# Input projection, third column pair as a seven-product block, and the attention spread over fewer units

## The chip, the cores and the metric

The kernel runs on one core of a Trainium2 chip. Its engines are TensorE (PE, the matmuls), VectorE (DVE), ScalarE (ACT), GpSimd (POOL) and SyncE (SP, which here only issues transfers); each works through its own instructions in order, and they wait for each other by semaphores. The metric is the time of one execution on the device in microseconds, lower is better.

## The reference

One encoder layer for 512 tokens of width 2048, all in float32:

```python
h = rmsnorm(x, g_mix)
qa, ka, va, qb, kb, vb = split(h @ w_in)          # 8 x 128, 2 x 128, 2 x 128, then three times 8 x 128
out_a = rmsnorm(mixer_a(qa, ka, va, g_q_a, g_k_a), g_out_a)   # 8 query heads on 2 kv heads, q/k normed, rotary
out_b = rmsnorm(mixer_b(qb, kb, vb), g_out_b)                 # 8 heads, three dilated windows, partial rotary
x = x + concat(out_a, out_b) @ w_out              # 2048 x 2048
h2 = rmsnorm(x, g_ffn)
x = x + (silu(h2 @ w_gate) * (h2 @ w_up)) @ w_down            # 5632 wide
return rmsnorm(x, g_final)
```

## The kernel before

**Number format.** A float32 product is made of three matmuls: each operand is split into a high part (ACT copies it to the 128x512 fp32r tile) and a low part (DVE subtracts the high part from the source), and `mm3` (L238 to L240) multiplies high by high, high by low and low by high. So each weight tile costs ACT and DVE one operation each, and those of DVE must be done before PE comes to the tile.

**Units.** The program is a list of units, one per weight tile, and the main loop issues them in order: it loads tiles ahead, splits some ahead, issues the unit's matmuls, then hooks that hang on that unit, and then tasks from a queue called `side`. Two kinds of unit occur in the part of concern. A plain unit (`in_chunk`, weights called `w`) takes 128 rows of the weights by 512 columns against all four groups of 128 tokens: 12 matmuls, 16 units for a chunk of 512 columns. A block unit (`ColBlock`, weights called `tw`) belongs to a scheme of seven products that computes a pair of chunks with 7/8 of the multiplications: 8 pairs of row groups x 7 products = 56 units of 6 matmuls, where two plain chunks would take 32 units of 12. A block needs sums and differences of raw weight tiles, which DVE makes (L825), and evicts its results in parts which are added up.

**Order of the program.** 16 units of a first chunk (kvA), block 1 (qA0, qA1, units 16 to 71), block 2 (vB0, vB1, units 72 to 127), then four plain chunks qkB0 to qkB3 (units 128 to 191), each with 256 columns of q and 256 of k of two B heads; then the output projection of the A heads (out A, 4 chunks of 8 units, 192 to 223) and of the B heads (out B, 224 to 255), then the feed-forward blocks, three quarters of the time. The chunk results that attention needs later go to DRAM (`store`) and are read back (`reload`, `load_vB`).

**Attention** has no units of its own. `attention_tasks` makes a queue of some 140 tasks with costs, in one order: the rotary tables (L410, L416), the q ropes of heads 0 to 3 (`norm_rope`, L432 to L449, on DVE), the split of vA (L492), the k ropes, then head 0's q transposes (L547) and the k transposes (L500), and then the slots. A slot (`head_slot`) is one step of a pipeline over heads: the score of 128 queries (three matmuls, L238 to L240 on `qT`), the norm of the slot before, the transposes of four p tiles six slots behind (L594, split into `pTh` and `pTl`), the exponential, and the product with v eight slots behind. The A heads take slots 0 to 31, the B heads 32 to 63. The q ropes of heads 4 to 7 hang on slots 6 to 9. How fast the queue is drained is set by numbers:

```python
credit = credit + HEAD_RATE[n >= attend[1]] if attend[0] <= n < attend[2] else 1.0
while side and credit >= getattr(side[0], "cost", 1.0):
    f = side.popleft()
    credit -= getattr(f, "cost", 1.0)
    f()
```

Before, `HEAD_RATE` gives 1.42 per unit beside the plain chunks and 1.9 beside out A. An A slot costs 1.5 and a B slot 1.2, so that up to two fit into a unit now and then. Eight PSUM banks are handed out in rotation (`bank`, `release`): a score of an A head keeps its bank until the exponential has read it, one of a B head until one DVE operation has, and the p transposes keep theirs until `pTl` is written (L230).

The o tiles of the A heads and of six B heads are stored to DRAM (`o_dram`) and read back by `Back` beside the first output chunk; the other B heads' are split by `early` just ahead of the units that use them. The arena holds the operands of the seven-product scheme; parts of it are reused by name (`place(m, i)`) when a form is no longer read.

Of the kernel before, what the change touches and what calls it, by code (L numbers as in the profile page):

```python
# [47 lines left out]
PLAIN_WAIT = 5  # L48
SPILL_B = 6
TWINS = 8  # L50
# [5 lines left out]
EVICT = 6  # L56
HEAD_RATE = (1.42, 1.9)
TURN_LAG = 6
VALUE_LAG = 8
COLUMN_BLOCKS = 2  # L60

# [6 lines left out]
def encoder_block(ctx, tc, x, g_mix, w_in, g_q_a, g_k_a, g_out_a, g_out_b, w_out, g_ffn,  # L68
# [31 lines left out]
    def release(*tiles):  # L100
        banks.extend(tiles)
# [54 lines left out]
    def place(m, i):  # L156
# [3 lines left out]
    O_HOMES = {"A": [(m, i) for i in range(6) for m in (5, 6)] + [(3, i) for i in range(4)],  # L160
               "B": [(m, i) for i in (6, 7) for m in range(7)]}

    load_x(0)
# [225 lines left out]
    def make_r1():  # L389
        ss = small()  # L390
        nc.vector.tensor_reduce(ss, x_ss.rearrange("p (t c) -> p t c", t=NT), axis=AX.X, op=OP.add)
        r1["r"] = rsqrt_mean(ss, NT, D)
        r1["rs"] = small()
        nc.vector.tensor_scalar(r1["rs"], r1["r"], HD ** -0.5, None, op0=OP.mult)

# [67 lines left out]
    def row_scale_of(name):  # L463
        return r1["rs" if name[:2] == "qB" else "r"]

    def post_plain(name, ps, rows=range(NT)):
        for t in rows:
            e = homes.popleft() if name == "kvA" else slot("ev" + name)
            if name[:3] == "qkB":
                nc.scalar.activation(e[:, :256], ps[t][:, :256], AF.Copy, scale=r1["rs"][:, t:t + 1])  # L470
                nc.scalar.activation(e[:, 256:], ps[t][:, 256:], AF.Copy, scale=r1["r"][:, t:t + 1])
            else:
                nc.scalar.activation(e, ps[t], AF.Copy, scale=1.0 if name == "kvA" else r1["r"][:, t:t + 1])
            release(ps[t])
            store(name, t, e)
            if name == "kvA":
                homes.append(e)
# [33 lines left out]
    def split_vB(h):  # L511
        vB[h] = split(vB[h].rearrange("p t c -> p (t c)"), "v")

    turn = [0]

    def rope_partial(q0, t):
# [4 lines left out]
        for s in range(2):  # L521
# [7 lines left out]
    o_dram = {(g, h): dp.tile([P, 512], F32, tag=f"o{g}{h}", name=f"o{g}{h}")  # L529
              for g, n in (("A", NHA), ("B", SPILL_B)) for h in range(n)}  # L530
    acc = {}
    heads = []

    class Head:
# [5 lines left out]
        def tq(self):  # L540
            ps = bank()
            for t in range(NT):
                if self.kind == "A":
                    src = qA[self.h // 4][t][:, (self.h % 4) * HD:(self.h % 4 + 1) * HD]
                else:
                    src = qkB[self.h // 2][t][:, (self.h % 2) * HD:(self.h % 2 + 1) * HD]
                nc.tensor.transpose(ps[:, t * P:(t + 1) * P], src, ident)  # L547
            self.q = split(ps, "qT")
            release(ps)

        def tk(self):
            if self.kind == "A":
                self.k = kTA[self.h // (NHA // NKV)]
                return
            ps = bank()
            for t in range(NT):
                lo = 256 + (self.h % 2) * HD
                nc.tensor.transpose(ps[:, t * P:(t + 1) * P], qkB[self.h // 2][t][:, lo:lo + HD], ident)
            self.k = split(ps, "kT")
            release(ps)  # L560

        def score(self, t):
# [46 lines left out]
        def fin(self):  # L609
            o = slot("oT")  # L610
            nc.scalar.activation(o, self.o, AF.Copy)
            oT[self.kind, self.h] = o
            if self.kind == "A" or self.h < SPILL_B:
                nc.gpsimd.dma_start(o_dram[self.kind, self.h], o)
# [178 lines left out]
    class ColBlock:  # L793
        def __init__(self, w, row, lo, pairs, plan, tag, ready=None, close=None, chain=CHAIN, apart=False):
# [6 lines left out]
            def raw(i, j, q):  # L801
                at = row + (2 * q + i) * P
                return Raw(lambda t: [(w[0, at:at + P, lo[j]:lo[j] + 512], t)], tag=tag, width=512)
            kinds = {"a": (0, 0), "b": (0, 1), "c": (1, 1), "d": (1, 0), "e": (0, 1), "f": (1, 0), "g": (1, 1)}
# [93 lines left out]

    def in_plain(name, lo):
        pieces = [(QB + 256 * lo, 0, 256), (KB + 256 * lo, 256, 256)] if name[:3] == "qkB" else [(lo, 0, 512)]  # L900
        in_chunk(pieces, lambda ps, rows: post_plain(name, ps, rows))

    first_chunk(1024, lambda ps: post_plain("kvA", ps))
    groups = [(("qA0", "qA1"), (0, 512)), (("vB0", "vB1"), (VB, VB + 512)), (("qkB0", "qkB1"), (0, 1)),
              (("qkB2", "qkB3"), (2, 3))]
    for names, lo in groups[:COLUMN_BLOCKS]:
# [24 lines left out]
    def out_chunk(kind, c):  # L931
# [4 lines left out]
        def early(k):  # L936
            if (kind, k) not in oS:
                drain_until(lambda: (kind, k) in oT)
                oS[kind, k] = split(oT.pop((kind, k)), "oS", go[:, base + k:base + k + 1],
                                    at=O_HOMES["B"][2 * k:2 * k + 2] if k < 7 else None)  # L940

# [29 lines left out]
        def post(rows):  # L971
# [9 lines left out]
            if kind == "B" and NT - 1 in rows:  # L981
# [10 lines left out]
                for i in (2 * c, 2 * c + 1):  # L992
# [3 lines left out]
        add_chunk(w_out, [(base + k) * P for k in order], [(c * 512, 0, 512)], mm, None,  # L996
                  early if kind == "B" else None,
                  (lambda k: [Back(k)] if kind == "A" or k < SPILL_B else []) if c == 0 else None, tag="wa" if kind == "A" else "wo")

# [429 lines left out]
```

## Time and profile before

| | |
|---|---|
| three runs, median | 1996.75 us (1995.93 to 1997.94) |
| the profiled execution | 1996.41 us, of which its trace spans 1994.6 |
| PE busy | 1978.2 us (99%) |
| DVE, ACT, POOL busy | 1560.1, 1108.2, 146.8 us |
| moved to and from DRAM | 390.62 MB, mean 196 GB/s |

Times in the profile are in microseconds from the span's start. In a row of a timeline stand the start, the duration, the engine, the line, the operation, what it writes and reads with the tile's size, and in brackets how long the engine had been idle and on what it waited. Matmuls are pipelined: a row's duration is longer than the distance to the next one, and the distance is what a matmul costs. Rows by stretch give the busy time of engines between two points in time. The units of block 2 end at 212.56 us, the first p is transposed at 274.1, and the last result of the plain chunks goes to DRAM from 466.5.

### The profile page before, as it was taken

The page shows a single profiled execution, that of the slowest core. Times are in us where ns is not written, and L with a number is a line of the kernel's source. Part 1 is how long each engine was busy: PE and PEld are TensorE (multiplying, and loading weights), DVE is VectorE, ACT ScalarE, POOL GpSimd, SP SyncE. Part 2 cuts the span into 40 slices and gives each one's busy share as a digit, 9 for nine tenths or more (in the row PEclk, how much of TensorE's full clock was granted, in tenths as well). Part 3 has the DMA queues.
Part 4 walks back from the last instruction along what each step waited for, and adds up shares of the span by engine and source line. Part 5 has one row for each costly group of instructions (what it writes and reads, how often), then busy time and mean ns, then how long its engine had stood idle before and what let it go on. Part 6 is the DMA issues. An engine that isn't in the chain of part 4 may idle for free. (4 is left out here: it accounts for less than half of the span.)

```text
span 1994.6 us, 27480 instructions
## 1 busy us (share of the span) xinstructions
PE 1978.2 (99%) x9019; PEld 1631.7 (82%) x9019; DVE 1560.1 (78%) x2786; ACT 1108.2 (56%) x1984; POOL 146.8 (7%) x191
## 2 busy tenths in 40 slices
PE   9999999999999999999999999999999999999997
PEld 7888888888888888888888888888888888788886
DVE  6888866668845698877878877878779987887968
ACT  7655345546543565555554555545556666666655
POOL 0000111101110000000000000000000121111121
PEclk9999999999999999999999999999999999999999
DMA  8586532335353654845837647658458699768864
GB/s 276 180 279 233 174 122 94 111 118 195 100 174 100 212 180 166 288 145 214 287 117 257 236 141 277 201 181 282 151 199 279 193 247 269 196 167 269 196 171 156
DMA packets 229216, 390.62 MB, mean 196 GB/s; under 512 B 21408, under 2 KB 70352, under 8 KB 228944
## 3 DMA queue, kind: packets, MB, share of 16 engines
q1 hardware_dynamic: 204736, 325.87, 48.6%
q0 software_dynamic: 17680, 41.95, 9.3%
q10 hardware_dynamic: 6656, 21.05, 3.1%
q8 instruction: 70, 1.15, 0.2%
q14 instruction: 74, 0.61, 0.1%
HBM read 325.08 MB, written 63.70 MB: 195 GB/s over the span
## 5 line engine op out<-in xcount | busy, mean ns | idle before, releaser
L238 PE MATMUL b<-tw,arena 128*128 128x512 f32 x2136 | 837.9, 392 | 2.2 <-ACT ev L1168 2.2
L239 PE MATMUL b<-tw,arena 128*128 128x512 f32 x2136 | 832.5, 390 | 1.9 <-DVE tw L788 1.8
L240 PE MATMUL b<-tw,arena 128*128 128x512 f32 x2136 | 832.4, 390 | 0.0
L785 ACT ACTIVATE tw<-raw 128x512 fp32r<-128x512 f32 x924 | 559.1, 628 | 437.0 <-DVE raw L825 283.9
L788 DVE TENSOR_TENSOR tw<-raw,tw 128x512 fp32r<-128x512 f32 x924 | 620.8, 689 | 171.4 <-ACT tw L785 168.2
L239 PEld LDWEIGHTS b<-tw,arena 128*128 128x128 f32 x2136 | 401.5, 188 | 86.3 <-DVE tw L788 4.8
L238 PEld LDWEIGHTS b<-tw,arena 128*128 128x128 f32 x2136 | 401.3, 188 | 84.7 <-ACT ev L1168 3.2
L240 PEld LDWEIGHTS b<-tw,arena 128*128 128x128 f32 x2136 | 401.0, 188 | 84.1
L825 DVE TENSOR_TENSOR raw<-raw,raw 128x512 f32<-128x512 f32 x528 | 363.3, 688 | 1.1 <-DMA raw<-in_w_gate_up_dram 1.0
L1169 POOL DMA_DIRECT2D x1d<-ev x76 | 66.4, 976 | 1149.0 <-ACT ev L1168 1144.2
L238 PE MATMUL b<-w,arena 128*128 128x512 f32 x368 | 146.4, 398 | 0.0
L240 PE MATMUL b<-w,arena 128*128 128x512 f32 x368 | 143.8, 391 | 0.0
L239 PE MATMUL b<-w,arena 128*128 128x512 f32 x368 | 143.4, 390 | 0.0
L229 ACT ACTIVATE pTh<-b 128x512 fp32r<-128x512 f32 x64 | 38.4, 599 | 117.5 <-PE b L594 114.9
L240 PEld LDWEIGHTS b<-w,arena 128*128 128x128 f32 x368 | 69.1, 188 | 15.1
L239 PEld LDWEIGHTS b<-w,arena 128*128 128x128 f32 x368 | 69.2, 188 | 14.0
L785 ACT ACTIVATE tw<-stage 128x512 fp32r<-128x512 f32 x96 | 58.0, 628 | 40.2 <-DVE stage L825 32.7
L238 PEld LDWEIGHTS b<-w,arena 128*128 128x128 f32 x368 | 69.1, 188 | 13.6
L788 DVE TENSOR_TENSOR tw<-stage,tw 128x512 fp32r<-128x512 f32 x96 | 64.2, 688 | 12.2 <-ACT tw L785 12.1
L295 DVE TENSOR_TENSOR w<-raw,w 128x512 fp32r<-128x512 f32 x96 | 66.1, 696 | 6.6 <-ACT w L290 4.0
L290 ACT ACTIVATE w<-raw 128x512 fp32r<-128x512 f32 x96 | 58.5, 626 | 14.7 <-PE b L240 6.9
L359 DVE TENSOR_TENSOR pair<-pair 128x256 f32<-128x256 f32 x120 | 45.5, 421 | 26.7 <-ACT pair L1025 25.6
(196 smaller groups left out, 1768.1 us busy)
## 6 DMA issues: line engine op xcount, KB each, us to landing
raw<-in_w_gate_up_dram SPq DMA_DIRECT2D x616, 256.0 KB, 5.4
raw<-in_w_down_dram SPq DMA_DIRECT2D x176, 256.0 KB, 6.6
stage<-in_w_in_dram SPq DMA_DIRECT2D x112, 256.0 KB, 5.3
forms<-pair SPq DMA_DIRECT2D x22, 896.0 KB, 5.3
x1d<-ev POOLq DMA_DIRECT2D x76, 256.0 KB, 6.8
fr<-forms ACTq DMA_DIRECT2D x35, 512.0 KB, 4.8
raw<-in_w_in_dram SPq DMA_DIRECT2D x64, 256.0 KB, 5.0
raw<-in_w_out_dram SPq DMA_DIRECT2D x32, 512.0 KB, 4.4
```

The lines of the kernel that those rows point to most:

```text
L229: nc.scalar.activation(hi, src, AF.Copy)
L238: nc.tensor.matmul(dst, ah, bh, start=start, stop=False, skip_group_check=chained)
L239: nc.tensor.matmul(dst, ah, bl, start=False, stop=False, skip_group_check=chained)
L240: nc.tensor.matmul(dst, al, bh, start=False, stop=stop, skip_group_check=chained)
L290: nc.scalar.activation(self.w[0], src, AF.Copy)
L295: nc.vector.tensor_tensor(self.w[1], self.src, f32(self.w[0]), op=OP.subtract)
L359: nc.vector.tensor_tensor(out, x, y, op=op)
L785: nc.scalar.activation(self.pair[:, 0], self.src, AF.Copy)
L788: nc.vector.tensor_tensor(self.pair[:, 1], self.src, f32(self.pair[:, 0]), op=OP.subtract)
L825: nc.vector.tensor_tensor(t[dst], t[src[0]], t[src[1]], op=OP.add if form == "m6" else OP.subtract)
L1169: nc.gpsimd.dma_start(x1_dram[2 * cb + j, row], e, accum_op=OP.add)
```

## The change

The third pair of chunks, qkB0 and qkB1, becomes a third block (units 128 to 183), and only qkB2 and qkB3 stay plain (units 184 to 215); out A follows in units 216 to 247 and out B from 248. Attention starts behind block 3, and its rates become 2.4 for 36 units (the plain pair and, by `ATTEND_PAST`, four units of out A) and 1.3 from there to four units into out B. A block's raw may now be loaded in pieces (256 columns of q, 256 of k), and the B heads' q scale moves from the eviction to the split of the turned q. Turned q and k and the v of the B heads from head 2 on go to fixed places of the arena (`HEAD_HOMES`). Of the A heads too only six are stored and read back, heads 6 and 7 are split from where they are.

```diff
-SPILL_B = 6
+SPILLED = 6
...
-HEAD_RATE = (1.42, 1.9)
+HEAD_RATE = (2.4, 1.3)
 TURN_LAG = 6
 VALUE_LAG = 8
-COLUMN_BLOCKS = 2
+COLUMN_BLOCKS = 3
+ATTEND_PAST = 4
...
+    HEAD_HOMES = {"q": [[(4, 0), (4, 1)], [(4, 2), (4, 3)]], "k": [[(2, 4), (2, 5)], [(4, 4), (4, 5)]],
+                  "v": [[(3, 4), (3, 5)], [(2, 0), (2, 1)]]}
...
-        r1["rs"] = small()
-        nc.vector.tensor_scalar(r1["rs"], r1["r"], HD ** -0.5, None, op0=OP.mult)
...
-            if name[:3] == "qkB":
-                nc.scalar.activation(e[:, :256], ps[t][:, :256], AF.Copy, scale=r1["rs"][:, t:t + 1])
-                nc.scalar.activation(e[:, 256:], ps[t][:, 256:], AF.Copy, scale=r1["r"][:, t:t + 1])
-            else:
-                nc.scalar.activation(e, ps[t], AF.Copy, scale=1.0 if name == "kvA" else r1["r"][:, t:t + 1])
+            nc.scalar.activation(e, ps[t], AF.Copy, scale=1.0 if name == "kvA" else r1["r"][:, t:t + 1])
...
-        vB[h] = split(vB[h].rearrange("p t c -> p (t c)"), "v")
+        vB[h] = split(vB[h].rearrange("p t c -> p (t c)"), "v", at=heads[NHA + h].home("v"))
...
-            self.q = split(ps, "qT")
+            self.q = split(ps, "qT", HD ** -0.5 if self.kind == "B" else None, at=self.home("q"))
...
-            self.k = split(ps, "kT")
+            self.k = split(ps, "kT", at=self.home("k"))
...
+        def home(self, part):
+            return HEAD_HOMES[part][self.h % 2] if self.kind == "B" and self.h > 1 else None
...
-            if self.kind == "A" or self.h < SPILL_B:
+            if self.h < SPILLED:
                 nc.gpsimd.dma_start(o_dram[self.kind, self.h], o)
...
-                return Raw(lambda t: [(w[0, at:at + P, lo[j]:lo[j] + 512], t)], tag=tag, width=512)
+                pieces = lo[j] if isinstance(lo[j], list) else [(lo[j], 0, 512)]
+                return Raw(lambda t: [(w[0, at:at + P, c:c + n], t[:, dst:dst + n]) for c, dst, n in pieces],
+                           tag=tag, width=512)
...
-    groups = [(("qA0", "qA1"), (0, 512)), (("vB0", "vB1"), (VB, VB + 512)), (("qkB0", "qkB1"), (0, 1)),
-              (("qkB2", "qkB3"), (2, 3))]
+    heads_b = [[(QB + 256 * n, 0, 256), (KB + 256 * n, 256, 256)] for n in range(4)]
+    groups = [(("qA0", "qA1"), (0, 512)), (("vB0", "vB1"), (VB, VB + 512)), (("qkB0", "qkB1"), heads_b[:2]),
+              (("qkB2", "qkB3"), heads_b[2:])]
...
         def early(k):
-            if (kind, k) not in oS:
+            if (kind, k) not in oS and k >= SPILLED:
                 drain_until(lambda: (kind, k) in oT)
                 oS[kind, k] = split(oT.pop((kind, k)), "oS", go[:, base + k:base + k + 1],
-                                    at=O_HOMES["B"][2 * k:2 * k + 2] if k < 7 else None)
+                                    at=O_HOMES[kind][2 * k:2 * k + 2] if kind == "A" or k < 7 else None)
...
-                  early if kind == "B" else None,
-                  (lambda k: [Back(k)] if kind == "A" or k < SPILL_B else []) if c == 0 else None, tag="wa" if kind == "A" else "wo")
+                  early if kind == "B" or c == 0 else None,
+                  (lambda k: [Back(k)] if k < SPILLED else []) if c == 0 else None, tag="wa" if kind == "A" else "wo")
...
         if kind == "A":
-            attend.append(len(units))
+            attend.append(len(units) + ATTEND_PAST)
+    attend[1] += ATTEND_PAST
```

How this moves instructions is seen at three places. First PE where the q transposes of head 0 (from `qA`) and the k transposes (from `kvA`) stand; `b_` are PSUM banks, `w_` split weights, `arena` the turned x. Before, the q transposes follow on the eleventh plain unit, and one more unit of 12 matmuls stands between them and the k transposes:

```order
L547 MATMUL b_75<-fixed,qA_25_1818 128x128 x4
L238 MATMUL b_77<-w_2020,arena_86 128x512
L239 MATMUL b_77<-w_2021,arena_86 128x512
L240 MATMUL b_77<-w_2020,arena_86 128x512
L238 MATMUL b_78<-w_2020,arena_86 128x512
L239 MATMUL b_78<-w_2021,arena_86 128x512
L240 MATMUL b_78<-w_2020,arena_86 128x512
L238 MATMUL b_72<-w_2020,arena_86 128x512
```

After, in the seventh plain unit behind block 3, the k transposes stand directly behind the q transposes (the line numbers of the changed file are three higher or lower):

```order
L241 MATMUL b_76<-w_2522,arena_85 128x512
L242 MATMUL b_76<-w_2523,arena_85 128x512
L243 MATMUL b_76<-w_2522,arena_85 128x512
L544 MATMUL b_72<-fixed,qA_25_2429 128x128 x4
L497 MATMUL b_73<-fixed,kvA_2464 128x128 x4
L497 MATMUL b_77<-fixed,kvA_2464 128x128 x4
```

What moved: PE comes to the k transposes after 84 plain matmuls instead of 144.

Second DVE, in the k ropes that those transposes read (`ra` and `smalls` are scratch, `gsk` and `gck` the tables). Before, from the first k rope's end into the second, with a weight split between:

```order
L440 TENSOR_TENSOR ra_2008<-kvA_1844,gsk_120 128x4x32 x2
L447 TENSOR_TENSOR kvA_1844<-kvA_1844,gck_119 128x256
L448 TENSOR_TENSOR kvA_1844<-kvA_1844,ra_2008 128x256
L449 TENSOR_TENSOR kvA_1844<-kvA_1844,smalls 128x256
L295 TENSOR_TENSOR w_1994<-raw_1826,w_1993 128x512
L432 ISA ra_2035,smalls<-kvA_1844 128x128
```

After, at the same place, the second rope follows at once:

```order
L441 TENSOR_TENSOR ra_2565<-kvA_2464,gsk_118 128x4x32 x2
L448 TENSOR_TENSOR kvA_2464<-kvA_2464,gck_117 128x256
L449 TENSOR_TENSOR kvA_2464<-kvA_2464,ra_2565 128x256
L450 TENSOR_TENSOR kvA_2464<-kvA_2464,smalls 128x256
L433 ISA ra_2576,smalls<-kvA_2464 128x128
```

What moved: from the first table operation to the last k rope DVE's instructions hold five weight splits instead of ten; the others are the same.

Third PE in the slots of the A heads. Before, one slot in a plain unit: the score (`qT`), the transposes of p, the product with v (`pT`), and then weights again:

```order
L238 MATMUL b_76<-arena_86,qTh_2752 128x512
L239 MATMUL b_76<-arena_86,qTh_2752 128x512
L240 MATMUL b_76<-arena_86,qTl_2753 128x512
L594 MATMUL b_78<-fixed,p_2732 128x128
L594 MATMUL b_78<-fixed,p_2786 128x128
L594 MATMUL b_78<-fixed,p_2821 128x128
L594 MATMUL b_78<-fixed,p_2859 128x128
L238 MATMUL b_74<-pTh_2908,arena_86 128x512
L239 MATMUL b_74<-pTl_2909,arena_86 128x512
L240 MATMUL b_74<-pTh_2908,arena_86 128x512
L238 MATMUL b_72<-w_2882,arena_86 128x512
```

After, in unit 202, a second slot follows on the first:

```order
L594 MATMUL b_74<-fixed,p_2776 128x128
L594 MATMUL b_74<-fixed,p_2811 128x128
L594 MATMUL b_74<-fixed,p_2819 128x128
L594 MATMUL b_74<-fixed,p_2863 128x128
L241 MATMUL b_71<-pTh_3051,arena_86 128x512
L242 MATMUL b_71<-pTl_3052,arena_86 128x512
L243 MATMUL b_71<-pTh_3051,arena_86 128x512
L544 MATMUL b_77<-fixed,qA_66_2755 128x128 x4
L241 MATMUL b_74<-arena_86,qTh_2952 128x512
L242 MATMUL b_74<-arena_86,qTh_2952 128x512
L243 MATMUL b_74<-arena_86,qTl_2953 128x512
L594 MATMUL b_76<-fixed,p_2776 128x128
```

What moved: the second slot's score goes to bank b_74, in which the first slot's transposed p still stands, with no weights between. Units 202 and 207 look like this; in 203, 205, 209, 211 and 213 it is the second slot's transposes of p that take that bank.

More of the change, by code (lines that the diff above doesn't have):

```diff
@@ L463, in row_scale_of @@
     def row_scale_of(name):
-        return r1["rs" if name[:2] == "qB" else "r"]
+        return r1["r"]
     def post_plain(name, ps, rows=range(NT)):
@@ L529, in encoder_block @@
     o_dram = {(g, h): dp.tile([P, 512], F32, tag=f"o{g}{h}", name=f"o{g}{h}")
-              for g, n in (("A", NHA), ("B", SPILL_B)) for h in range(n)}
+              for g, n in (("A", SPILLED), ("B", SPILLED)) for h in range(n)}
     acc = {}
@@ L897, in encoder_block, with in_plain @@
     blocks, ends = [], []
-    def in_plain(name, lo):
-        pieces = [(QB + 256 * lo, 0, 256), (KB + 256 * lo, 256, 256)] if name[:3] == "qkB" else [(lo, 0, 512)]
+    def in_plain(name, pieces):
         in_chunk(pieces, lambda ps, rows: post_plain(name, ps, rows))
     first_chunk(1024, lambda ps: post_plain("kvA", ps))
-    groups = [(("qA0", "qA1"), (0, 512)), (("vB0", "vB1"), (VB, VB + 512)), (("qkB0", "qkB1"), (0, 1)),
-              (("qkB2", "qkB3"), (2, 3))]
+    heads_b = [[(QB + 256 * n, 0, 256), (KB + 256 * n, 256, 256)] for n in range(4)]
+    groups = [(("qA0", "qA1"), (0, 512)), (("vB0", "vB1"), (VB, VB + 512)), (("qkB0", "qkB1"), heads_b[:2]),
+              (("qkB2", "qkB3"), heads_b[2:])]
     for names, lo in groups[:COLUMN_BLOCKS]:
```

## The prediction, made before the changed kernel had run

> **What bounds the kernel now.** I read the page's busy times first, then the waits of PE, then busy times by stretch, then the timelines of PE and DVE where the third column pair ends in the new order.
>
> ```profile
> PE 1978.2 (99%) x9019; PEld 1631.7 (82%) x9019; DVE 1560.1 (78%) x2786; ACT 1108.2 (56%) x1984; POOL 146.8 (7%) x191
> ...
> PE b L238 <- ACT ev L1168: 2.2, 2, 1.7
> PE b L239 <- DVE tw L788: 1.8, 5, 0.6
> PE b L174 <- DVE warm L168: 1.3, 1, 1.3
> PE b L186 <- DMA stage<-in_g_mix_dram: 0.8, 1, 0.8
> ...
> 136.30:212.50 76.20, 76.20 (x338) 63.10 (x337) 60.68 (x103) 36.18 (x60) 4.88 (x9) 1.00 0.70 233
> 212.50:245.80 33.30, 33.30 (x151) 27.52 (x151) 31.81 (x113) 11.17 (x22) 7.28 (x8) 1.00 0.41 138
> 245.80:450.00 204.20, 204.20 (x996) 169.07 (x995) 133.97 (x316) 99.24 (x218) 22.91 (x29) 1.00 0.34 112
> ```
>
> PE is busy 99% of 1994.6 us. The list of waits (total, times, longest) is complete, and adds up to 6.1. The rows by stretch give length, then PE, weight loads, DVE, ACT and POOL busy, PE clock, DMA share and GB/s: the second seven-product block (vB), the start of attention, and the rest of the plain chunks with most of the A heads. PE is full in all three, but in the second DVE is busy 31.81 of 33.30: there the cover is thin, and the change works exactly on it.
>
> **Removed: 48 matmuls.** Two plain chunks are 32 units of 12 matmuls (384), a block is 56 units of 6 (336). What one costs on PE follows from the start of attention:
>
> ```profile
> 212.56 0.39 PE L238 MATMUL b<-w,arena 128*128 128x512 f32 x1
> ...
> 242.49 0.60 PE L547 MATMUL b<-fixed,qA 128*128 128x128 f32 x4
> 242.84 0.48 PE L238 MATMUL b<-w,arena 128*128 128x512 f32 x1
> ...
> 245.68 1.04 PE L500 MATMUL b<-fixed,kvA 128*128 128x128 f32 x8
> ```
>
> From 212.56 (I call it T0, the end of the block) to the q transposes stand 11 units, 132 matmuls, in 29.93 us: 0.2268 each. The 48 are worth -10.9 us wherever PE is full.
>
> **Block 3 itself.** It is laid out as block 2, whose row shows PE without a gap, DVE at 60.68 of 76.20 and ACT at 36.18. The new tw splits, raw sums and ends closes (DVE +56, +32, +6; ACT +56, +8) sit in that slack, and I cost them at nothing. If it were gone, PE would wait, as now it does 1.8 us on tw. The q scale moved into the split of turned q, the freed arena homes and A6/A7 kept instead of stored and reloaded change operands, not durations; their cover is DVE's slack of 70 us in the 204.20 row.
>
> Its weights come as two 128 KB issues per raw, 112 on SP, in rows of half the length. Nearest rows:
>
> ```profile
> stage<-in_w_in_dram SPq DMA_DIRECT2D x112, 256.0 KB, 5.3
> ...
> raw<-in_w_in_dram SPq DMA_DIRECT2D x64, 256.0 KB, 5.0
> ```
>
> The first is the loads of the two blocks, the second includes the half-width ones of the plain qkB chunks: the same landing time, 5.0 against 5.3, and loads are issued up to 20 us ahead. With the DMA share at 0.70 I cost this at nothing; if it were late, PE would wait on tw for the excess over 20 us.
>
> **Moved: the start of attention.** The rate goes from 1.42 to 2.4 of task cost per unit. The table, q rope, v split and k rope work of DVE is the same, but PE reaches the k transposes after 7 plain units instead of 12. PE issues in order; the weights behind the transposes don't help it. The chain on DVE before:
>
> ```profile
> 205.74 1.30 DVE L295 TENSOR_TENSOR w<-raw,w 128x512 fp32r<-128x512 f32 x2 [0.70 <-ACT w L290]
> 209.56 0.69 DVE L295 TENSOR_TENSOR w<-raw,w 128x512 fp32r<-128x512 f32 x1 [2.53 <-DMA vB<-ends]
> 210.17 0.89 DVE L416 SCALAR_TENSOR_TENSOR gsk<-ctab,turning 128x128 f32<-128x128 f32 x4
> ...
> 231.50 0.48 DVE L492 SCALAR_TENSOR_TENSOR arena<-kvA,smalls,arena 128x256 fp32r<-128x256 f32 x1
> 231.90 0.68 DVE L295 TENSOR_TENSOR w<-raw,w 128x512 fp32r<-128x512 f32 x1
> 232.50 1.27 DVE L492 SCALAR_TENSOR_TENSOR arena<-kvA,smalls,arena 128x256 fp32r<-128x256 f32 x3
> ...
> 245.47 0.43 DVE L449 TENSOR_TENSOR kvA<-kvA,smalls 128x256 f32<-128x256 f32 x1
> ...
> 210.17:245.81 35.64, 34.15 (x121) 1.00 0.45 154
> 213.71:231.50 17.79, 17.09 (x60) 1.00 0.60 203
> ```
>
> The last two rows are DVE alone by stretch: the whole chain, 34.15 busy in 35.64, and in it the q ropes. Before, the last k rope starts at 245.47 and the transposes at 245.68: they meet, with no slack. Ten weight splits stand between (0.60 each, from 231.90 to 232.50), of which the changed order has five there. So the chain from 210.17 to 245.68, 35.5 us, becomes 32.5. If it begins at T0-2.4 as now, it ends at T0+30.1. PE is there at T0 + 84 x 0.2268 + 0.43 = T0+19.5 (0.43 is the q transposes with the hand-over, 245.68 less 242.49 less 12 matmuls). The wait is 10.6. The lower bound: DVE stood idle 2.53 at 209.56, for a spill's store to land, and 0.70 before; without these it starts 3.2 earlier, and 7.4 are left. I take 10.6, since the new block ends with the same stores, as near a row as there can be. Behind the waiting transposes stand weight matmuls and the first score; nothing else is late, since DVE's splits for them are in the chain.
>
> **The clock after that wait.** Nowhere in this trace does PE stand idle for 10 us. The nearest rows are its start:
>
> ```profile
> 1.26 2.74 PE L174 MATMUL b<-warm 128*128 128x512 bf16 x6 [1.26 <-DVE warm L168]
> ...
> 8.02 0.63 PE L239 MATMUL b<-tw,arena 128*128 128x512 f32 x1
> 8.44 0.63 PE L240 MATMUL b<-tw,arena 128*128 128x512 f32 x1
> 8.87 0.55 PE L238 MATMUL b<-tw,arena 128*128 128x512 f32 x1
> 9.26 0.39 PE L239 MATMUL b<-tw,arena 128*128 128x512 f32 x1
> 9.49 0.39 PE L240 MATMUL b<-tw,arena 128*128 128x512 f32 x1
> ...
> 0.00:9.20 9.20, 7.15 (x21) 4.32 (x22) 1.82 (x5) 4.35 (x8) 0.92 (x5) 1.00 0.81 246
> ```
>
> Matmuls come 0.42 apart until 8.87 and 0.23 apart from 9.26, though the granted clock reads 1.00 throughout. From the first at 1.26 that is 8 us at half pace, a loss of at most 4.0; at the other end, none, if 10 us of idleness don't bring this back. I take the middle, 2.0.
>
> The Trainium skill ("TensorE: Matmul & The Clock Gate", Part 1: The HAM clock gate) says that the array drops to half rate after an idle window of about 3.4 us and regains full rate after about 3.4 us of sustained work, which speaks against this change. The rows at the trace's start agree in kind. By the rule the loss would be 1.7 (an estimate, half of 3.4) and the sum +5.6 instead of +5.9.
>
> **The second q ropes.** The tasks for heads 4 to 7, 15.4 of DVE work (17.79 less four splits), fall into five units at the new rate. With each operation at its row's duration these units (operations counted in the changed order) hold 24.0 us for DVE and 20.5 for PE, so DVE falls 3.5 behind. Cover is what DVE idles before a score's reduction, 2.09 in the row below; 1.4 is left. Bounds 0 and 3.5.
>
> **Two A slots in one unit.** At 2.4, seven units take two slots with a transposed p (before, no A unit did). One slot, before:
>
> ```profile
> 341.77 0.39 PE L238 MATMUL b<-arena,qTh 128*128 128x512 f32 x1
> ...
> 342.45 0.60 PE L594 MATMUL b<-fixed,p 128*128 128x128 f32 x4
> 342.65 0.69 DVE L570 TENSOR_REDUCE smalls<-b 128x1 f32<-128x512 f32 x1 [2.09 <-PE b L240]
> ...
> 343.09 0.60 ACT L229 ACTIVATE pTh<-b 128x512 fp32r<-128x512 f32 x1 [2.78 <-PE b L594]
> ...
> 343.59 0.39 PE L238 MATMUL b<-w,arena 128*128 128x512 f32 x1
> ...
> 343.85 0.69 DVE L230 TENSOR_TENSOR pTl<-b,pTh 128x512 fp32r<-128x512 f32 x1
> ```
>
> The slot takes PE 1.82 us (341.77 to 343.59); the bank of its p transposes comes free when pTl ends, 2.77 after the slot's start. The second slot takes that bank: for its score where q transposes (0.35) stand between (two units), 0.60 too early; for its own p transposes otherwise (five), 2.50 after the start, 0.27 too early. 2 x 0.60 + 5 x 0.27 = 2.6, with 0.04 for each hand-over (342.45 + 0.60 to ACT's 343.09) some 2.8. Bounds 0, and 7.6 if one more DVE operation of 0.69 stands ahead of each pTl.
>
> **Sum.** -10.9 + 10.6 + 2.0 + 1.4 + 2.8 = +5.9, on the profiled execution's 1996.41: 2002.3. The median of the runs is 0.34 above that execution, so 2002.6. The bounds add up to -3.5 and +14.8. Behind the first 36 units I cost nothing: at 1.3 per unit a slot of 1.2 or 1.5 comes at most once in a unit, and at 1.9, where six units of before took two B slots, PE shows no wait on DVE but the 1.8 on tw.
>
> **Rivals.**
> 1. *The pairs bind.* DVE is one operation late at each: +4.8, 2007.4. For it: DVE is already behind from the q ropes. Against: in these units DVE has less work than PE (4.0 to 6.0 against 6.3 to 6.8, operations at their rows' durations).
> 2. *Not slower: DVE's chain starts early.* At the block's end the raw slot that DVE waits for comes free 2.5 us sooner; the wait is 7.4 and the sum +2.7, 1999.4. For it: 3.2 us of idleness in front of the chain. Against: the changed order has the same wait on a store there. It decides from a start at T0-4.3: then the sum is below 4.0, which is 0.2%, about what a measurement tells from no change.
> 3. *Nothing but the start-up counts.* Clock stays, ropes and pairs are covered: -0.3, 1996.4.
> 4. *2 and 3 together:* -3.5, 1993.2, close to the edge of faster (-4.0).
> 5. *The change doesn't do what it says:* not possible for the matmuls; the changed order has 48 fewer on PE.
>
> **How the numbers follow.** Chances: forecast 0.38, rival 1 0.20, rival 2 0.16, rival 3 0.12, rival 4 0.14. Slower is the forecast and rival 1, less 0.02 for a forecast with small terms: 0.56. Faster is the part of rival 4 beyond 0.2%: 0.08. Within 0.2%: 0.36. The range leaves out the lower part of rival 4 and the upper end of all bounds: 1994.0 to 2010.5; the forecast's own is 2000.7 to 2006.
>
> **What would show it.** One PE wait of about 10 us on DVE at the transposes of kvA, some 20 us after the last tw matmul; matmuls 0.42 apart right behind it; waits under a microsecond of scores or p transposes on pTl in the units with two slots; 48 fewer matmuls. I am wrong if the wait is under 7 or in several places, if block 3 itself shows PE waits on raw or tw, or if the waits behind the start add up to over 13.

## The result, and the profile after

The changed kernel takes 2008.29 us (median of four runs, 2007.35 to 2009.75) against 1996.34 for the kernel before: a ratio of 1.0056, 95% interval 1.0043 to 1.0069. It is slower by some 12 us; the forecast was 2002.6, with a range of 1994.0 to 2010.5. All medians and ratios here are over executions in the fast state: single executions of 7168 and 6264 us, of two of the kernels below, are left out.

The profiled executions span 2008.0 and 1994.6, so 13.4 us are to be explained (that execution of the changed kernel is the slowest of its four, 1.5 above their median). First the page's busy times and the whole list of what PE waited for in the changed kernel (engine, tile and line, what it waited for: total, times, longest):

```profile
PE 1973.4 (98%) x8971; PEld 1624.4 (81%) x8971; DVE 1597.1 (80%) x2847; ACT 1121.6 (56%) x1992; POOL 145.2 (7%) x187
...
PE b L497 <- DVE kvA L450: 6.6, 3, 2.8
PE b L242 <- DVE w L298: 5.3, 3, 2.5
PE b L594 <- DVE pTl L233: 4.0, 4, 2.1
PE b L241 <- ACT ev L1171: 2.2, 2, 1.7
PE b L241 <- DVE smalls L574: 2.0, 1, 2.0
PE b L177 <- DVE warm L171: 1.3, 1, 1.3
PE b L241 <- DVE pTl L233: 0.8, 2, 0.4
PE b L242 <- DVE tw L788: 0.8, 3, 0.3
PE b L189 <- DMA stage<-in_g_mix_dram: 0.3, 1, 0.3
```

There are 48 matmuls fewer in the records (8971 against 9019), and the waits add up to 23.3 us, where they were 6.1. All that is new waits for DVE. By stretch (length; busy PE, weight loads, DVE, ACT, POOL; clock, DMA share, GB/s) it stands in the first 90 us behind the third block, which ends at 287.60:

```profile
287.60:319.96 32.36, 21.98 (x98) 17.29 (x96) 30.70 (x112) 8.52 (x18) 7.29 (x8) 0.95 0.32 112
319.96:345.00 25.04, 25.04 (x111) 20.48 (x110) 15.94 (x38) 10.69 (x25) 0.00 (x0) 0.93 0.32 105
345.00:380.00 35.00, 29.61 (x145) 23.58 (x144) 30.56 (x84) 16.08 (x33) 7.32 (x9) 1.00 0.25 83
380.00:450.00 70.00, 68.75 (x343) 55.45 (x343) 47.57 (x106) 37.79 (x83) 8.00 (x9) 1.00 0.29 101
```

In the first row DVE is busy 30.70 of 32.36 and PE is idle for a third. In the second the clock is 0.93: that is the half pace behind the wait. In the third, the second q ropes, DVE is busy 30.56 of 35.00. The timeline of PE through the first two:

```profile
301.20 0.39 PE L241 MATMUL b<-w,arena 128*128 128x512 f32 x1
304.11 0.50 PE L242 MATMUL b<-w,arena 128*128 128x512 f32 x1 [2.52 <-DVE w L298]
304.44 0.40 PE L243 MATMUL b<-w,arena 128*128 128x512 f32 x1
...
308.41 0.50 PE L242 MATMUL b<-w,arena 128*128 128x512 f32 x1 [1.29 <-DVE w L298]
...
313.39 0.33 PE L497 MATMUL b<-fixed,kvA 128*128 128x128 f32 x1 [1.64 <-DVE kvA L450]
316.49 0.33 PE L497 MATMUL b<-fixed,kvA 128*128 128x128 f32 x1 [2.77 <-DVE kvA L450]
318.98 1.33 PE L497 MATMUL b<-fixed,kvA 128*128 128x128 f32 x5 [2.16 <-DVE kvA L450]
319.96 0.78 PE L241 MATMUL b<-w,arena 128*128 128x512 f32 x1
320.53 0.63 PE L242 MATMUL b<-w,arena 128*128 128x512 f32 x1
...
323.52 0.40 PE L243 MATMUL b<-w,arena 128*128 128x512 f32 x1
323.76 0.40 PE L241 MATMUL b<-w,arena 128*128 128x512 f32 x1
```

The idleness is 10.4 us in five pieces: twice the low part of a weight is late (2.52, 1.29), and then each k rope in turn holds up its own transposes (1.64, 2.77, 2.16), since PE goes on with one token group while DVE ropes the next. Behind it matmuls come 0.43 apart until 323.52. A stop costs more than its idle time: from 301.20 to the second matmul behind the wait, at 304.44, 3.24 us pass, where two matmuls take 0.45; 2.79 are lost and 2.52 are named as idle. So this stop has some 0.27 of restart on top (some 0.2 where transposes stand behind the wait), and I put 0.27 on each. On DVE the chain begins and ends as before, in front of it the same wait for a spill to land:

```profile
285.00 0.69 DVE L298 TENSOR_TENSOR w<-raw,w 128x512 fp32r<-128x512 f32 x1 [2.93 <-DMA qkB<-ends]
285.61 0.89 DVE L417 SCALAR_TENSOR_TENSOR gsk<-ctab,turning 128x128 f32<-128x128 f32 x4
...
318.50 0.42 DVE L450 TENSOR_TENSOR kvA<-kvA,smalls 128x256 f32<-128x256 f32 x1
```

It starts at the block's end less 2.0 (forecast 2.4) and takes 33.4 to the transposes at 318.98 (forecast 32.5).

The sum, by the traces: -10.9 (48 matmuls), +10.4 (the start), +2.0 (half pace behind it), +5.0 (second q ropes: 1.45, 2.08, 1.46), +1.3 (pairs: 0.40, 0.40, 0.27, 0.24), +2.0 (one wait of a B score at 464.65, for the operation that frees its bank: two B ropes, a split of a read-back o and a weight's low part stand ahead of that on DVE), +1.6 (a second stretch at half pace, below), -1.5 (waits on tw and g_mix that are shorter here), and 13 stops of 0.27 = 3.5. That makes 13.4, but not as exactly as it looks: the list leaves out waits under 0.15 us, and four more pairs of A slots have one. There the p transposes start 0.54 behind the last matmul of the second slot's score instead of 0.23, a loss of 0.31 each:

```profile
385.09 0.40 PE L243 MATMUL b<-arena,qTl 128*128 128x512 f32 x1
385.63 0.66 PE L594 MATMUL b<-fixed,p 128*128 128x128 f32 x4
```

With these 1.2 the terms overshoot by as much, so the account closes to about 1 us.

The second stretch at half pace is in the last feed-forward part. Before and after, PE waits there for one eviction; before (1.68 us at 1714.72) the pace stayed full, after it did not:

```profile
1726.13 0.58 PE L241 MATMUL b<-tw,arena 128*128 128x512 f32 x1 [1.66 <-ACT ev L1171]
1726.50 0.63 PE L242 MATMUL b<-tw,arena 128*128 128x512 f32 x1
...
1729.88 0.40 PE L241 MATMUL b<-tw,arena 128*128 128x512 f32 x1
```

All fourteen traces of this case have this wait, of 1.66 to 1.68, and only three of them the half pace behind it. So these 1.6 come of this execution rather than of the change.

### The profile page after: what moved, and what is told of

Same layout as the page of the kernel before. It is cut to its first block, busy times and chain, and to the rows that moved or that the text cites. A ratio compares the mean times of both kernels' runs of the same rounds, so it can differ in the third digit from the quotient of the medians.

```text
span 2008.0 us, 27642 instructions
## 1 busy us (share of the span) xinstructions
PE 1973.4 (98%) x8971; PEld 1624.4 (81%) x8971; DVE 1597.1 (80%) x2847; ACT 1121.6 (56%) x1992; POOL 145.2 (7%) x187
## 5 line engine op out<-in xcount | busy, mean ns | idle before, releaser
L241 PE MATMUL b<-tw,arena 128*128 128x512 f32 x2248 | 881.5, 392 | 2.2 <-ACT ev L1171 2.2
L242 PE MATMUL b<-tw,arena 128*128 128x512 f32 x2248 | 876.4, 390 | 0.9 <-DVE tw L788 0.8
L243 PE MATMUL b<-tw,arena 128*128 128x512 f32 x2248 | 876.4, 390 | 0.0
L242 PEld LDWEIGHTS b<-tw,arena 128*128 128x128 f32 x2248 | 422.6, 188 | 89.3 <-DVE tw L788 2.9
L243 PEld LDWEIGHTS b<-tw,arena 128*128 128x128 f32 x2248 | 422.4, 188 | 89.0 <-DVE arena L335 0.4
L241 PEld LDWEIGHTS b<-tw,arena 128*128 128x128 f32 x2248 | 422.6, 188 | 88.8 <-ACT ev L1171 3.1
L785 ACT ACTIVATE tw<-stage 128x512 fp32r<-128x512 f32 x143 | 86.8, 628 | 63.3 <-DVE stage L827 43.5
L788 DVE TENSOR_TENSOR tw<-stage,tw 128x512 fp32r<-128x512 f32 x143 | 95.6, 686 | 18.4 <-ACT tw L785 18.3
L242 PE MATMUL b<-w,arena 128*128 128x512 f32 x240 | 94.6, 394 | 5.3 <-DVE w L298 5.3
L241 PE MATMUL b<-w,arena 128*128 128x512 f32 x240 | 96.5, 402 | 0.0
L243 PE MATMUL b<-w,arena 128*128 128x512 f32 x240 | 94.3, 393 | 0.0
L1171 ACT ACTIVATE ev<-b,smalls 128x512 f32<-128x512 f32 x76 | 49.7, 683 | 28.0 <-PE b L243 26.8
L1075 DVE TENSOR_TENSOR s<-b,s 128x512 f32<-128x512 f32 x66 | 44.0, 688 | 24.7 <-PE b L243 24.7
L242 PEld LDWEIGHTS b<-w,arena 128*128 128x128 f32 x240 | 45.6, 190 | 15.6 <-DVE w L298 6.5
L243 PEld LDWEIGHTS b<-w,arena 128*128 128x128 f32 x240 | 45.5, 189 | 10.0
L1103 ACT ACTIVATE pair<-b 128x512 f32<-128x512 f32 x44 | 26.3, 597 | 47.9 <-PE b L1100 47.5
```

Source lines behind the costliest of these rows:

```text
L241: nc.tensor.matmul(dst, ah, bh, start=start, stop=False, skip_group_check=chained)
L242: nc.tensor.matmul(dst, ah, bl, start=False, stop=False, skip_group_check=chained)
L243: nc.tensor.matmul(dst, al, bh, start=False, stop=stop, skip_group_check=chained)
L785: nc.scalar.activation(self.pair[:, 0], self.src, AF.Copy)
L788: nc.vector.tensor_tensor(self.pair[:, 1], self.src, f32(self.pair[:, 0]), op=OP.subtract)
L1075: nc.vector.tensor_tensor(d[:, t], box.bank_of(form)[t], d[:, t], op=OP.add)
```

## The experiments

Theory 1: the loss is where DVE's chain of tables, ropes and splits is met too early, that is, a matter of the order. Theory 2: attention beside 32 fewer plain units is too much work for DVE wherever it is put.

**The fast start alone, without the third block.** The kernel before, with

```diff
+    def head_rate(n):
+        if n < attend[0] + 32:
+            return 2.4 if n < attend[0] + 8 else 1.09
+        return HEAD_RATE[n >= attend[1]]
...
-        credit = credit + HEAD_RATE[n >= attend[1]] if attend[0] <= n < attend[2] else 1.0
+        credit = credit + head_rate(n) if attend[0] <= n < attend[2] else 1.0
```

> The kernel before with only the start of attention changed: 2.4 per unit for 8 units, 1.09 for 24, then as before. Theory 1: the k transposes come after 84 matmuls as in the changed kernel, with the same chain of DVE ahead of them, so the same loss of 10.4 us idle, 1.3 of restarts and 1.7 of half clock: 2008 to 2011. If the loss at the start needs the third block (its transfers or its last splits on DVE), the time stays at 1996 to 2000.

Measured: 2007.29 us, ratio 1.0052 (1.0037 to 1.0067). Its PE waits for the k transposes and the weights ahead of them:

```profile
PE b L500 <- DVE kvA L449: 6.4, 3, 2.8
PE b L239 <- DVE w L295: 2.8, 2, 1.6
```

The 6.4 in three pieces is the changed kernel's 6.6, and behind it stands the same half pace (0.43 from one matmul to the next, from 243.19 to 247.03). Nothing of the block is needed for this loss: 9.2 us idle, five restarts (1.4), 2 of half pace (12.6), of which the span shows 10.6. In this execution waits on tw and g_mix are 1.6 shorter than in that of the kernel before; the rest of the difference is not traced.

**The slow start.** The changed kernel, with 1.42 for the first 12 units, 2.4 up to four units into out A, and 1.6 then:

```diff
+    def head_rate(n):
+        if n < attend[0] + 12:
+            return 1.42
+        return 2.4 if n < attend[1] else 1.6
```

> Theory 1 (the loss stands where DVE's chain of tables, ropes and splits is met too early): at 1.42 for the first 12 units, then 2.4, then 1.6, the waits at the start (10.4 us idle in five pieces, some 0.3 more for each restart, 1.7 of half clock: 13.4 together) go, and the time falls to about 1995 to 1998; the waits at the second q ropes stay. Theory 2 (DVE's work over all 36 units is the bound, wherever it is put): what is saved at the start comes back later, and the time stays at 2004 to 2009.

Measured: 1999.83, ratio 1.0019 (1.0009 to 1.0029); the profiled execution spans 1996.6. PE's list has no wait on `kvA` or `w` any more; its longest entries on DVE:

```profile
PE b L241 <- DVE pTl L233: 3.5, 5, 1.5
PE b L594 <- DVE pTl L233: 2.9, 4, 2.1
...
PE b L241 <- DVE smalls L574: 1.4, 1, 1.4
```

The start's loss is gone by the order alone, as theory 1 has it: 7 to 8 us less than the changed kernel, though not down to the 1995 to 1998 expected. The kernel is still no faster than before: with the same 48 matmuls saved, 8.5 us of waits in 12 places are left or new, 6.4 of them on pTl.

**The rates of before.** Third block and all else as changed, but

```diff
+    def head_rate(n):
+        if n < attend[0] + 0:
+            return 1.42
+        return 1.42 if n < attend[1] else 1.9
```

> The block alone: third block and all else as changed, but the rates of before (1.42 up to four units into out A, 1.9 then), with what is left of attention (some 13 of 125 in cost) drained in out B. Theory 1: no wait at the start nor at the second q ropes, nearly the whole 10.9 us of the 48 matmuls is gained, less what the B heads' last slots wait in out B: 1988 to 1994. If the block itself costs time, in any of its parts, it stays above 1997.

Measured: 2002.21, ratio 1.0029 (1.0017 to 1.0041). I had missed by 8 us. There is no wait at the start nor at the first slots up to 381 us. From there to 430, before out A begins at 431, PE waits 3.2, and from 430 to 500 another 8.5, all on DVE:

```profile
PE b L241 <- DVE pTl L233: 3.5, 5, 1.5
PE b L594 <- DVE pTl L233: 3.3, 7, 1.9
PE b L242 <- DVE pTl L233: 2.4, 1, 2.4
...
PE b L241 <- DVE smalls L574: 1.9, 3, 1.4
```

The block itself is not what costs: PE's list has no wait between 69 us and 381. So its gain can't be had by leaving attention at its old pace: the 64 slots have 68 units to stand in (184 to 251) where they had 96 (128 to 223). Why they wait at rates at which the kernel before has no such wait is not shown.

**Sums of squares on ACT.**

```diff
+            sq = slot("rj")
             for h in range(nh):
-                nc.vector.tensor_tensor_reduce(tmp[:, h * HD:(h + 1) * HD], q0[:, h * HD:(h + 1) * HD],
-                                               q0[:, h * HD:(h + 1) * HD], 1.0, 0.0, op0=OP.mult, op1=OP.add,
-                                               accum_out=ss[:, h:h + 1])
+                nc.scalar.activation(sq[:, h * HD:(h + 1) * HD], q0[:, h * HD:(h + 1) * HD], AF.Square,
+                                     accum_out=ss[:, h:h + 1])
```

> The sums of squares of all q and k ropes go from DVE to ACT: some 1.0 us less of DVE for a q rope and 0.5 for a k rope, 6 us of the first chain and 4 of the second q ropes. Theory 1: the waits at the start fall from 10.4 to some 4.5, those at the second q ropes from 5.0 to some 2, the half clock goes in part: 1996 to 2000. Rival: ACT, now in the chain, is late with them or with the weights' high parts: 2004 or more.

Measured: 2005.59, ratio 1.0045 (1.0030 to 1.0060), some 6 above what theory 1 gave. The idleness at the start falls to 5.7 (0.16, 1.30, 0.47, 2.19, 1.59), near to what was expected, but the waits at the second q ropes stay (1.32, 1.66, 1.46 against 1.45, 2.08, 1.46): less work on DVE there helps by 0.6 in all; in two of the three the p transposes wait for a pTl that still stands behind a whole rope. ACT isn't what PE waits for, so the rival's time came without its cause. Of the 4.7 saved at the start the time shows 2 to 3.

**The second q ropes, one per slot.**

```diff
-            at(6 + n // 2, [f])
+            at(4 + n, [f])
```

> The second q ropes hang on slots 4 to 11, one per slot, instead of two on each of slots 6 to 9. Theory 1: their three waits (5.0 us idle, 0.8 of restarts) fall to some 1 to 2: about 2004. Theory 2: DVE's backlog is the same and the waits only move: 2007 to 2009.

Measured: 2006.33, ratio 1.0049 (1.0034 to 1.0064), about 2 less than the changed kernel, with overlapping intervals, and between the two theories. Of the three waits of 5.0 two are left, of 0.59 and 2.06. The slow start and this together:

> The slow start of the first experiment (1.42 for 12 units, 2.4 for 24, 1.6 then) and the second q ropes one per slot. Theory 1: to the first experiment's profile (no wait at the start, some 8.5 us idle in 13 places behind it) it takes away the 2.8 at the second q ropes, so some 3 us less than it: about 1996. Theory 2: the same time as the slow start alone, with the waits elsewhere.

Measured: 2000.24, ratio 1.0021 (1.0011 to 1.0031): not to be told from the slow start alone. Its waits at the second q ropes are 1.07, 1.98, 2.03 and 0.45, together 5.5, where the slow start alone has 2.8. So spreading them did not help here: the waits moved and grew, and theory 1's 1996 was missed.

**PE kept busy while it waits.** 84 transposes of the identity ahead of the k transposes:

```diff
+KEEP = 84
...
         ps = bank()
+        if kv == 0:
+            for _ in range(KEEP):
+                nc.tensor.transpose(ps[:, :P], ident, ident)
```

> 84 transposes of the identity ahead of the k transposes keep PE busy while it waits for DVE; nothing else changes. If the half pace behind the wait comes of the idleness, matmuls behind it run at 0.23 from the first, and the time falls by 1.6 to 2, to about 2006.5. If the half pace comes of something else, the time stays within 0.5 of the changed kernel's 2008.3, or rises by what the transposes overrun.

Measured: 2008.73, ratio 1.0058 (1.0043 to 1.0073), no difference in time. The timeline of PE tells why:

```profile
310.44 9.33 PE L499 MATMUL b<-fixed 128*128 128x128 f32 x84
319.61 1.04 PE L501 MATMUL b<-fixed,kvA 128*128 128x128 f32 x8
320.41 0.47 PE L242 MATMUL b<-w,arena 128*128 128x512 f32 x1
...
320.95 0.40 PE L244 MATMUL b<-w,arena 128*128 128x512 f32 x1
```

Matmuls behind it run at 0.23 from the first, and the granted clock of this stretch is 1.00, so the half pace did come of the idleness. But the transposes took 9.2 us (0.109 each, where four q transposes take 0.35), while DVE's last k rope had ended at 317.86; by overrunning 1.75 they gave back what the pace had gained. In time the price of the half pace is therefore not shown; by the spacing in the trace it is 2.0 (7 matmuls and five transposes at double length).

**Shorter chain, later start, spread ropes.** The edits for ACT and for the second q ropes, and

```diff
+    def head_rate(n):
+        if n < attend[0] + 9:
+            return 1.87
+        return 2.2 if n < attend[1] else 1.55
```

> Sums of squares on ACT, the second q ropes one per slot, rates 1.87 for 9 units, 2.2 for 27, 1.55 then. The chain is 6 us shorter and met 2 units later than in the changed kernel, so waits at the start under 2 us; those behind it, which are pairs of slots and B heads, as in the slow start, 4 to 6 us: 1992 to 1996. If ACT's squares are late, 1998 or more.

Measured: 2001.85, ratio 1.0026 (1.0017 to 1.0036). 2.6 us of waits at the k transposes are left, and behind them the same kind of waits as in the slow start. The expected 1992 to 1996 was missed by 6. DVE's busy time fell by some 9 us (1597.1 to 1588.3). Behind the start PE waits 5.8 on attention, as expected (4 to 6), where the slow start has 8.5; but with a weight's 0.9 the start waits 3.5 instead of under 2, and tw 2.2 instead of 0.9. Why the time is no better than that of the slow start is not traced further.

**Two half portions per unit.** What all of these still have is that slots of one unit follow each other on PE. Here attention's tasks are issued after 6 of a unit's 12 matmuls and at its end, at half the rate each; rates and ropes are those of the slow start with spread ropes:

```diff
             for t in range(NT):
                 product(k, u.w, t)
+                if t == 1:
+                    drain_half(u.at)
...
             for i, w in both:
                 product(i, w, t)
+            if t % 2 == 0:
+                drain_half(u.at)
...
+    def drain_half(n):
+        if attend[0] <= n < attend[2]:
+            credit[0] += head_rate(n) / 2
+            drain()
```

> As the kernel with the slow start and the spread q ropes, but attention's tasks are issued twice in a plain unit or output unit, after 6 of its 12 matmuls and at its end, with half the rate each time: two slots of a unit then have six matmuls (1.36 us of PE) between them. If what is left behind the start is that a second slot follows on the first (its bank, its pTl), the 8.5 us idle and the restarts go down to 2 to 4 us: 1990 to 1994. If what is left is DVE's amount of work in too few units, the waits move and the time stays at 1997 to 2001.

Measured: 1993.63, ratio 0.9983 (0.9974 to 0.9992): 6.6 us less than the same kernel with whole portions, and a little faster than the kernel before. Its waits on pTl, by p transposes and by scores, and the one that has come at the k transposes:

```profile
PE b L594 <- DVE pTl L233: 2.5, 5, 1.1
...
PE b L497 <- DVE kvA L450: 1.2, 1, 1.2
...
PE b L241 <- DVE pTl L233: 0.7, 2, 0.4
```

With whole portions they were 2.5 and 4.3 on pTl and 1.5 on a B score. DVE has the same work in nearly the same units (1599.8 us busy against 1596.6); only where the tasks stand within a unit is new. That decides for the order and against DVE's amount of work, for much of what is left behind the start. Ropes and splits move by up to half a unit too, so it does not show that the distance between slots alone does it. At other rates:

```diff
-        if n < attend[0] + 12:
-            return 1.42
-        return 2.4 if n < attend[1] else 1.6
+        if n < attend[0] + 10:
+            return 1.7
+        return 2.2 if n < attend[1] else 1.7
```

> The same with rates 1.7 for 10 units, 2.2 up to four units into out A and 1.7 then: DVE's chain at the start is met 2 units earlier (a wait of some 4 us there), and fewer slots fall into the plain pair. If pairs were what cost time, 1993 to 1997; if DVE's amount of work is the bound, 1998 to 2003.

Measured: 1998.22, ratio 1.0004 (0.9995 to 1.0013), by the median in the range that I had given to DVE's amount of work. But the start is met two units earlier and waits 4.8 there (3.6 on the ropes, 1.2 on a weight); the waits behind it are the smallest of all (1.6 on pTl). What is gained behind the start is lost there. At the rates of the slow start again, with the edit that puts the squares on ACT:

> The kernel with half-unit issue and spread q ropes, and the sums of squares on ACT: 9.9 us less work for DVE in the first 24 units. If the wait of 1.2 at the k transposes and those of some 2 at the p transposes beside the second q ropes are DVE's work, they go, and the time falls by 2 to 4 us below 1993.6, to 1990 to 1992. If ACT, now ahead of DVE in more places, is what they meet, 1993 to 1996.

Measured: 1994.69, ratio 0.9990 (0.9981 to 0.9999), not to be told from the kernel without it; the 1990 to 1992 were missed. The wait at the k transposes is gone, but 4.2 on pTl and 1.7 on tw stand against 3.2 and 1.0. PE waits for ACT no more than without the edit. And, without that edit, with a little slower start:

```diff
-            return 1.42
-        return 2.4 if n < attend[1] else 1.6
+            return 1.36
+        return 2.4 if n < attend[1] else 1.65
```

> The same without ACT's squares, but with 1.36 per unit instead of 1.42 for the first 12 units and 1.65 instead of 1.6 at the end: the k transposes come half a unit later, and the wait of 1.2 there with its restart goes: 1992 to 1993. If a later start costs as much in the B heads' slots as it saves, 1993.5 to 1995.

Measured: 1992.61, ratio 0.9980 (0.9972 to 0.9989). The wait at the k transposes is 0.3. This is the fastest kernel here, 4 us below the kernel before and 15 below the changed one; its lead of 1 us over the one with 1.42 is within the intervals, and its waits on pTl are longer (5.2 against 3.2). Of the 10.9 us that the 48 matmuls are worth it keeps a little over a third.

## Why the prediction was right, and where its sizes were off

Slower was right, and for the reason given: a start met too early ate the gain of the 48 matmuls, and what came on top made it slower. The time lay within the range, but outside the forecast's own 2000.7 to 2006: it was +5.9, and the traces show +13.4, the medians 12.0. Nearest came rival 1 with 2007.4, by luck, as its cause (DVE one operation later at every pair) did not occur.

- **48 matmuls, -10.9.** The records are 48 fewer. That a matmul less is a matmul's time gained holds where PE is full, as the prediction said; no run shows it alone in the time, because none got rid of all waits.
- **Block 3 at nothing.** Right: PE's list has no wait on the new loads, and 0.8 on tw in all, less than the 1.8 of before and none of it in block 3 (66.85, 68.72 and 1708.80 us). Half-length rows of weights landed in time.
- **The start, 10.6.** Measured 10.4, and the fast start alone reproduces it without the block. Its place was not all right: "nothing else is late, since DVE's splits for them are in the chain" looks only behind the transposes, and 3.8 of the 10.4 is two weight splits that PE reaches ahead of them. And it came in five pieces, which is one of the prediction's own signs of being wrong ("in several places"), and each has its restart. This term was left out altogether, 3.5 over all 13 stops. With its restarts the start costs nearer 12 than 10.6, the chain having begun 0.4 later and taken 0.9 longer than forecast. (By its own rows the 0.43 of the q transposes is 0.47: 3.19 less 12 x 0.2268.)
- **The clock, 2.0.** Measured 2.0, by spacing; as the middle of 0 to 4.0 it is near by luck. The 1.00 that the prediction read at the start of the trace was no reading: in that trace the clock's record begins only at 9.19, where the pace doubles. That the pace would also drop elsewhere, at a wait that the kernel before has too, was not foreseen (1.6).
- **The second q ropes, 1.4 (0 to 3.5).** Measured 5.0 and the restarts of three stops: this is the term of the sum that was mis-sized most, beyond its own bound. The step that failed is the cover, "what DVE idles before a score's reduction". Those 2.09 us can't be drawn on while DVE is behind. The first wait (1.45 at 350.68) is for a weight's low part that stands behind a rope; in the other two the p transposes of a slot need the bank of the slot before, hence its pTl, and that stands on DVE behind whatever was issued ahead of it. The order of DVE around the wait of 2.08 shows it:

```profile
362.01 0.69 DVE L450 TENSOR_TENSOR qA<-qA,smalls 128x512 f32<-128x512 f32 x1
362.62 0.69 DVE L298 TENSOR_TENSOR w<-raw,w 128x512 fp32r<-128x512 f32 x1
363.23 0.68 DVE L570 TENSOR_REDUCE smalls<-b 128x1 f32<-128x512 f32 x1
...
364.42 0.68 DVE L233 TENSOR_TENSOR pTl<-b,pTh 128x512 fp32r<-128x512 f32 x1
```

- **The pairs, 2.8 (0 to 7.6).** Right for the A slots, in kind and nearly in size: all seven waited, the two with q transposes between their slots 0.40 each (0.65 by spacing; forecast 0.60), the others 0.27 once and 0.14 four times (0.43 and 0.31 by spacing; forecast 0.27). By spacing that is 3.0. Pairs of B slots were not priced. The first unit of out A, which starts at 457.49, has one, and its second slot waits 2.01 and 0.24, since B ropes and the split of a read-back o join the slots on DVE. With the start mended, waits on pTl at the slots are much of what is left, as the half portions show: 6.6 us. The row of the B score:

```profile
464.65 0.50 PE L241 MATMUL b<-kTh,qTh 128*128 128x512 f32 x1 [2.01 <-DVE smalls L574]
```

- **Nothing behind the first 36 units.** Right: that wait is in the 33rd of them, and from 466 us to the feed-forward part PE's list has none.
- **Rivals.** Rival 1 fell, for the changed kernel as it stands: the pairs were not one operation later. Rival 2 fell, as DVE's chain did not start early (2.0 before the block's end, where 4.3 was needed). Rival 3 fell, as the clock dropped and the ropes were not covered, and rival 4 with both.

What stays open: why the rates of before leave 18 us of waits (6 in the kernel before), place by place; and whether a schedule exists that gets the whole 10.9.

## What to carry to other kernels

Fewer matmuls on a full PE pay only if what PE covered keeps its cover: look for the stretch in which another engine is nearly as busy (here 31.81 of 33.30 us), and ask how many units of the main work stand ahead of each thing that PE must wait for. When an engine's busy share has room and PE still waits on it, ask what stands ahead of the awaited instruction in its queue: moving the same work by half a unit gained 6.6 us here, while taking some 9 us of work off DVE (1599.8 to 1591.0) gained nothing behind the start. Count the restart of each stop, and possibly a stretch at half pace, with the idle time itself.

## What the runs showed of the hardware

PE at half pace needs no long idleness. It came after 1.66 us of waiting (1726.13 in the changed kernel), and after 2.09 in the slow start, where it lasted from 363.64 to some 367.0:

```profile
363.64 1.12 PE L594 MATMUL b<-fixed,p 128*128 128x128 f32 x4 [2.09 <-DVE pTl L233]
```

In the kernel before, a wait of 1.68 us left the pace full. So a wait of this length may or may not cost some 1.6 us more. Rows by stretch show how. Of the changed kernel, the half clock at the start, the stretch around the wait at 1726.13, and the half clock behind it:

```profile
316.70:323.53 6.83, 4.67 (x15) 3.78 (x15) 5.19 (x13) 1.72 (x3) 0.70 (x1) 0.50 0.26 86
1723.00:1726.41 3.41, 1.73 (x6) 1.15 (x7) 3.41 (x6) 2.27 (x5) 0.00 (x0) 1.00 0.51 150
1726.41:1729.82 3.41, 3.41 (x9) 2.65 (x9) 3.22 (x6) 2.75 (x5) 1.76 (x2) 0.50 0.88 236
```

The stretch around the same wait in the kernel before, whose clock stays at 1.00 behind it:

```profile
1712.44:1715.86 3.42, 1.74 (x8) 1.13 (x7) 3.40 (x7) 2.85 (x6) 0.79 (x2) 1.00 0.71 230
```

In all fourteen traces the granted clock is either 1.00 or 0.50, and the stretches between its changes are whole multiples of 3.41 us: 3.41, 6.83 and 10.24 at half clock, 310.61 and 1402.88 at full. So the clock is set from one window of 3.41 us to the next, and the half clock can begin while PE still waits, as at 316.70, where the transposes went on at 318.98. How much work a window must hold is not shown: PE was busy 1.73 us in the one that lost the clock and 1.74 in the one that kept it.

The Trainium skill ("TensorE: Matmul & The Clock Gate", Part 1: The HAM clock gate) speaks of an idle window of about 3.4 us and the same time of work to come back. The time to come back agrees roughly (3.1 to 5.7 us here, from the end of the wait); the idle time doesn't, the gaps of 1.66 and 2.09 being about half as long. That the window runs freely, as it also says, fits the multiples of 3.41 and that equal gaps differ.
